# One encoder kernel: the front of each layer issued by a list scheduler in the builder, and group A's rope and softmax scaling moved to DVE

## The chip, the core and the metric

The kernel runs on one core of one Trainium2 chip. A core has five engines with queues of their own, each of which takes its instructions strictly in the order in which the built program puts them: PE (matrix multiplies, with the weight loads shown as PEld), DVE (element-wise work and reductions), ACT (activations and copies), POOL (element-wise work on SBUF alone) and SP (here the queue that issues the DMAs). Matrix products land in PSUM, which has eight banks of 128 x 512 f32; everything else lives in SBUF. The metric is the device time of one launch in microseconds (us); the time given for a kernel is the median of its runs.

## What is computed

Two layers of an encoder over 512 positions of width 1024, in f32. Each layer is a front (norm, projections, two kinds of attention, output projection) and a mixer (gated MLP with a short convolution):

```python
for l in range(DEPTH):                                   # 2 layers
    h = rmsnorm(x, g_attn[l])
    qa, ka, va, qb, kb, vb = split(h @ w_in[l])          # 1024 -> 2304 columns
    qa, ka, qb, kb = (rope(rmsnorm_per_head(t)) for t in (qa, ka, qb, kb))
    ya = windowed_gqa_sink(qa, ka, va, sink[l])          # group A: 8 q heads, 2 kv heads, +/-128 keys
    yb = diff_attention(qb, kb, vb, lam)                 # group B: 4 heads, two softmaxes each, all keys
    yb = rmsnorm(yb, subln[l]) * (1.0 - lambda_init)
    x = x + concat(ya, yb) @ w_out[l]
    h = rmsnorm(x, g_ffn[l])
    gate, val = split(h @ w_up[l])
    x = x + (silu(conv3(gate)) * val) @ w_down[l]
```

## The kernel before

**Products in three parts.** Every operand of a large product is held as a rounded high part and a low remainder, and `mm3` (L200) issues three matmuls for one product: high by high, high by low, low by high. A high part is made by a copy on ACT, the low part by a subtraction on DVE or POOL (`split`, L189; `split_out` for results that come from PSUM). Weights arrive as units of up to 512 KB: one DMA, one copy on ACT, one subtraction; units of the later projections and of the output projection have the subtraction on POOL, the first four projection chunks and the mixer on DVE. Up to three units are prepared ahead of their use.

**The front.** The input projection has nine chunks of 256 columns (`CHUNKS`): `akv`, `aq0`, `aq1` for group A, then `bq`, `bk`, `bv` for each half of group B. In `project` a chunk runs as two token pairs `tp` of 48 matmuls each (`pj_aq`, `pj_bq` ... in the profile). A finished q or k chunk goes through `qk_out`: ACT copies and squares (`raw`, `sq`), DVE reduces the squares (L354), POOL takes the reciprocal root (L245), the rotated half is multiplied (L366, on DVE for A and on POOL for B), POOL multiplies by the cosine table (L371) and adds (L372), DVE scales a k chunk (L374), and PE transposes into the one `tq` bank (`tr_ka`, `tr_qa`, `tr_bq`, `tr_bk`), from which high and low parts are made.

**Group A** has eight blocks (head pair `ip`, query block `qb`). `a_scores` makes two sets of scores (`sc_a`, PE), masks them and takes maxima on DVE (L451), then the exponentials (L469) and the scaling by the reciprocal sum (L476), both on ACT, into four `so_a` tiles of the eight `tmp` buffers. `a_values` transposes the probabilities (`pt_a`), splits them and multiplies by the values (`pv_a`).

**Group B** has 16 blocks (half, `qb`, head `j`). `b_scores` makes two sets of scores into the single two-bank buffer `sc` (`sc_b`), DVE takes the maxima (L539), ACT the two exponentials (L543), and DVE combines both maps into one (L547 to L551). `b_weights` transposes (`wt_b`) and splits (`wh_b`, `wl_b`), `b_values` multiplies by the values into the one `acc` bank (`yb`), and `b_norm` does the per-head norm of a pair of heads: a sum of squares on PE (`ss_yb`), a reciprocal root on POOL (`rr_yb`), a broadcast on PE (`rt_yb`), a multiplication on DVE (L603) and a split.

**The output projection** runs in passes as its inputs become ready: `out_pass(0)` over group A's rows (`wo`, 96 matmuls of 512 columns), `out_pass(1)` over the first half of B (48), and `out_last` over the second half of B in two token halves (`wo`, 48 matmuls of 256 columns each); the last of them, `out_last(1)`, cannot begin before the last `b_norm`.

**What sets the order.** `akv`, `aq0` and `aq1` run one after another. Then `weave` takes steps from two tracks, the attention (`attend`) and the rest (`proj_b(0)`, `proj_b(1)`, the output passes), so that both advance in proportion to two fixed totals, `ATT` = 92.0 and 98.6. Within `attend` the values of a block follow the scores of the next (group A) or next but one (`LAG` = 2, group B). The tile framework then sorts all instructions by priority against a modelled timeline of its own and writes each engine's queue; where the builder asks for it, `high_priority` moves group A's scores ahead.

## Time and profile before

| | us |
|---|---|
| median of 3 runs | 1272.37 (1271.11 to 1274.77) |
| the profiled execution | 1273.49 |
| its span in the trace | 1271.7 |
| PE, DVE, ACT, POOL busy in that span | 1228.0, 722.4, 573.5, 348.6 |

"Busy" counts a matmul from its start until its modelled end, and matmuls overlap, so that PE shows as busy while a short wait or a slower clock passes; the clock that PE was granted stands apart, as PEclk. A front begins in layer 0 at 19.2 us of the span, where the first `pj_aq` follows the chunk `akv` that was computed while `x` was loaded, and ends at 276.5 us, where the first `up` matmul starts. In layer 1 it goes from 640.4 us, the first `pj_akv`, to 904.6 us, the last `wo`.

### The profile page before, as it was taken

What the parts mean: (1) busy time and instruction counts of PE and PEld (TensorE: products, weight loads), DVE (VectorE), ACT (ScalarE), POOL (GpSimd) and SP (SyncE); (2) the same over time, 40 slices, a digit from 0 to 9 for tenths busy, and PEclk for the clock granted to TensorE, in tenths of its full rate; (3) what the DMA queues carried; (4) which work ended last, traced back from release to release, by engine and by line L of the source; (5) the groups of instructions that cost most, each with busy time, mean ns of one, the idle gap of its engine ahead of it and who ended that gap; (6) DMA issues with size and microseconds to landing.
All of it is one profiled execution on the core that took longest, in us unless ns stands there. A gap on an engine that the chain in (4) does not pass through costs nothing. (4 is left out here: it accounts for less than half of the span.)

```text
span 1271.7 us, 17055 instructions
## 1 busy us (share of the span) xinstructions
PE 1228.0 (97%) x6644; PEld 1035.9 (81%) x6644; DVE 722.4 (57%) x1186; ACT 573.5 (45%) x1011; POOL 348.6 (27%) x348
## 2 busy tenths in 40 slices
PE   9989997899999999999999899988999999999998
PEld 8879975688888888888898889867888888888887
DVE  6665677776655335554456667766865543355532
ACT  5487754444433223333444787554444332233321
POOL 1894641133111000112157647412321100011100
PEclk9999997999999999999999899979999999999999
DMA  6211220113332333322332212101133323333232
GB/s 210 68 51 51 59 67 17 34 51 100 106 95 82 100 107 106 91 89 84 106 89 62 66 35 67 51 17 50 50 116 99 100 75 99 108 99 100 81 110 91
DMA packets 33616, 102.92 MB, mean 81 GB/s; under 512 B 3968, under 2 KB 5248, under 8 KB 33536
## 3 DMA queue, kind: packets, MB, share of 16 engines
q1 hardware_dynamic: 33536, 101.84, 26.4%
q8 instruction: 52, 0.85, 0.3%
q14 instruction: 28, 0.23, 0.1%
HBM read 99.73 MB, written 2.10 MB: 80 GB/s over the span
## 5 line engine op out<-in xcount | busy, mean ns | idle before, releaser
L190 ACT CAST wh<-wr 128x1024 fp32r<-128x1024 f32 (+2 forms) x202 | 195.0, 967 | 401.6 <-PE up L202 171.4
L202 PE MATMUL up<-nf_l,wh 128*128 128x512 f32 x704 | 274.6, 390 | 0.6 <-DVE nf_l L220 0.5
L203 PE MATMUL up<-nf_h,wl 128*128 128x512 f32 x704 | 274.1, 390 | 0.4
L201 PE MATMUL up<-nf_h,wh 128*128 128x512 f32 x704 | 273.5, 390 | 0.0
L191 DVE TENSOR_TENSOR wl<-wr,wh 128x1024 fp32r<-128x1024 f32 (+2 forms) x166 | 185.5, 1118 | 105.9 <-ACT wh L190 105.6
L741 POOL TENSOR_TENSOR cv<-cv,rb 128x512 f32<-128x512 f32 x44 | 59.1, 1345 | 516.3 <-ACT cv L740 516.3
L202 PEld LDWEIGHTS up<-nf_l,wh 128*128 128x128 f32 x704 | 132.2, 188 | 30.0 <-DVE nf_l L220 2.8
L203 PEld LDWEIGHTS up<-nf_h,wl 128*128 128x128 f32 x704 | 132.2, 188 | 28.7 <-DVE wl L191 1.5
L201 PEld LDWEIGHTS up<-nf_h,wh 128*128 128x128 f32 x704 | 132.2, 188 | 27.3 <-ACT nf_h L219 0.2
L201 PE MATMUL dn<-act,wh 128*128 128x512 f32 x352 | 138.4, 394 | 0.0
L203 PE MATMUL dn<-act,wl 128*128 128x512 f32 x352 | 137.7, 392 | 0.0
L202 PE MATMUL dn<-act,wh 128*128 128x512 f32 x352 | 136.3, 388 | 0.0
L191 POOL TENSOR_TENSOR wl<-wr,wh 128x1024 fp32r<-128x1024 f32 x36 | 86.6, 2411 | 98.6 <-ACT wh L190 79.5
L734 DVE TENSOR_TENSOR gp<-up,rb 128x512 f32<-128x512 f32 x44 | 30.3, 692 | 104.1 <-PE up L203 98.8
L203 PEld LDWEIGHTS dn<-act,wl 128*128 128x128 f32 x352 | 66.1, 188 | 15.5
L202 PEld LDWEIGHTS dn<-act,wh 128*128 128x128 f32 x352 | 66.1, 188 | 14.8
L201 PEld LDWEIGHTS dn<-act,wh 128*128 128x128 f32 x352 | 66.2, 188 | 13.2
L742 DVE TENSOR_TENSOR cv<-cv,up 128x512 f32<-128x512 f32 x44 | 30.2, 686 | 81.1 <-POOL cv L741 71.8
L543 ACT ACTIVATE e_b<-sc_b,mx_b,rqb 128x512 f32<-128x512 f32 x64 | 49.3, 776 | 41.0 <-DVE mx_b L540 36.0
L755 DVE TENSOR_TENSOR x<-x,dn 128x512 f32<-128x512 f32 x32 | 22.1, 689 | 76.4 <-PE dn L203 76.4
L740 ACT ACTIVATE cv<-cv 128x512 f32<-128x512 f32 x44 | 27.7, 632 | 71.6 <-DVE cv L739 71.6
L539 DVE TENSOR_REDUCE mx_b<-sc_b 128x2 f32<-128x1024 f32 x32 | 39.0, 1220 | 10.0 <-PE sc_b L537 9.8
(224 smaller groups left out, 2545.3 us busy)
## 6 DMA issues: line engine op xcount, KB each, us to landing
wr<-w_up SPq DMA_DIRECT2D x88, 512.0 KB, 3.6
wr<-w_in SPq DMA_DIRECT2D x34, 512.0 KB, 3.7
wr<-w_down SPq DMA_DIRECT2D x32, 384.0 KB, 3.0
wr<-w_down SPq DMA_DIRECT2D x32, 320.0 KB, 2.9
wr<-w_out SPq DMA_DIRECT2D x16, 512.0 KB, 3.7
x<-xT SPq DMA_DIRECT2D x8, 256.0 KB, 4.4
outT<-x SPq DMA_DIRECT2D x8, 256.0 KB, 2.0
prob_f<-w_in SPq DMA_DIRECT2D x8, 128.0 KB, 4.3
```

The source lines that it names most:

```text
L190: nc.scalar.copy(hi, raw)
L191: eng.tensor_tensor(out=lo, in0=raw, in1=hi, op=ALU.subtract)
L201: nc.tensor.matmul(acc, lhsT=a[0], rhs=b[0], start=start, stop=False)
L202: nc.tensor.matmul(acc, lhsT=a[0], rhs=b[1], start=False, stop=False)
L203: nc.tensor.matmul(acc, lhsT=a[1], rhs=b[0], start=False, stop=stop)
L539: nc.vector.tensor_reduce(out=mx, in_=scp, axis=AX, op=ALU.max)
L543: nc.scalar.activation(e[c], sc[c], AF.Exp, bias=mx[:, c:c + 1], scale=rq[:, c:c + 1], accum_out=lsum[:, c:c + 1])
L734: nc.vector.tensor_tensor(out=g[:, 1:S + 1], in0=acc[0], in1=rb, op=ALU.mult)
L740: nc.scalar.activation(cv, cv, AF.Silu)
L741: nc.gpsimd.tensor_tensor(out=cv, in0=cv, in1=rb, op=ALU.mult)
L742: nc.vector.tensor_tensor(out=cv, in0=cv, in1=acc[1], op=ALU.mult)
L755: nc.vector.tensor_tensor(out=x_sb[d], in0=x_sb[d], in1=acc, op=ALU.add)
```

## The change

The front of each layer is put out by a list scheduler in the builder. A clock `clk` advances by an estimated time for each piece of PE work that a track yields; `pause` lets a track wait for an estimated time, `when` for names that `mark` has put a time to. Buffers of one kind are such names too: the score buffer (`sc`), the two transpose banks (`at0`, `at1`), `acc` and `tq`. `pump` always takes the ready track of the lowest rank. Chains behind a finished bank (`qk_out`, `a_soft`, `b_soft`, `copy_out`, `b_norm`, `add_x`) are spawned as tracks of rank 0, the values of all blocks are one track of rank 1, the scores of all blocks one of rank 2, and a track of rank 3, `filler`, holds all projections and output passes. So filler is issued only where nothing else is ready by the estimate. `proj_b(1)` starts once all of group A's scores are out.

Three things change beside the order. In `qk_out` group A's cosine product and addition go from POOL to DVE. In the softmax of A the four scalings go from ACT's `activation` to DVE's `tensor_scalar`. `wt_b` always uses the `at` banks, and the first projection pairs of a layer use the `mm` banks alone. The framework's own sorting stays on; the `high_priority` block is gone.

```diff
-    def weave(*tracks):
...
+    def when(*names):
+        return lambda: max(due.get(n, never) for n in names)
+
+    def mark(name, dt=0.0):
+        due[name] = clk["now"] + dt
+
+    def spawn(rank, gen):
+        tracks.append([rank, gen, lambda: 0.0])
+
+    def pump():
+        while tracks:
+            ready = [v for v in tracks if v[2]() <= clk["now"]]
+            if not ready:
+                clk["now"] = min(v[2]() for v in tracks)
+                assert clk["now"] < never
+                continue
+            tr = min(ready, key=lambda v: v[0])
+            step = next(tr[1], None)
+            if step is None:
+                tracks.remove(tr)
+            elif callable(step):
+                tr[2] = step
+            else:
+                clk["now"] += step
+                tr[2] = lambda: 0.0
...
-            rsqrt(rs, sv)
+            cv = tab[:, 0, t2].unsqueeze(2).broadcast_to([P, 2, nh, HD])
             tb = sq
+            eng = nc.vector if on_dve else nc.gpsimd
             for i in range(2):
...
-            cv = tab[:, 0, t2].unsqueeze(2).broadcast_to([P, 2, nh, HD])
-            nc.gpsimd.tensor_tensor(out=heads(raw), in0=heads(raw), in1=cv, op=ALU.mult)
-            nc.gpsimd.tensor_tensor(out=raw, in0=raw, in1=tb, op=ALU.add)
+            eng.tensor_tensor(out=heads(raw), in0=heads(raw), in1=cv, op=ALU.mult)
+            eng.tensor_tensor(out=raw, in0=raw, in1=tb, op=ALU.add)
+            rsqrt(rs, sv)
+            if on_dve:
+                yield pause(0.6 + 2.8 * n / CW)
+            else:
+                due["POOL"] = max(clk["now"] + 1.0, due["POOL"]) + 1.6 + 2.6 * n / CW
+                t = due["POOL"] + 0.2
+                yield lambda: t
...
             for i in range(4):
-                nc.scalar.activation(so[i][:, :n], so[i][:, :n], AF.Copy, scale=rl[:, i:i + 1])
+                nc.vector.tensor_scalar(out=so[i][:, :n], in0=so[i][:, :n], scalar1=rl[:, i:i + 1], scalar2=None,
+                                        op0=ALU.mult)
             a_so[ip, qb] = so
+            mark(f"so{ip}{qb}", 4 * (0.15 + 0.5 * n / S))
...
-        def attend():
...
+        def all_scores():
+            for ip, qb in a_seq:
+                yield from a_scores(ip, qb)
+            mark("a_scored")
+            for half, qb, j in b_seq:
+                yield from b_scores(half, qb, j)
...
         def proj_b(half):
+            if half:
+                yield when("a_scored")
...
+        def filler():
+            yield from first_part()
+            yield from proj_b(0)
+            yield from proj_b(1)
+            yield from out_pass(0, mm)
+            yield from out_pass(1, mm)
+            yield when("yb10")
             w_last.extend([next_unit(), next_unit()])
             yield from out_last(0, w_last, mm)
 
-        weave((attend(), ATT),
-              (chain(proj_b(0), proj_b(1), out_pass(0, mm), out_pass(1, mm), out_tail()), 98.6))
+        spawn(2, all_scores())
+        spawn(1, all_values())
+        spawn(3, filler())
+        pump()
         run(out_last(1, w_last, wide))
```

**PE, layer 0, group B's second half.** `sc_b_2_0` are the scores of head 2, query block 0; `wt_b_2_0` the transposes of its combined map. Before, the queue held at this place:

```order
L563 MATMUL wt_b_2_0_2568<-ident,e_b_2_0_0_2432 128x128 x4
L537 MATMUL sc_b_3_0_2528<-bkh_1_1607,bqh_1_1605 128x512 x2
L537 MATMUL sc_b_3_0_2528<-bkl_1_1608,bqh_1_1605 128x512 x2
L537 MATMUL sc_b_3_0_2528<-bkh_1_1607,bql_1_1606 128x512 x2
L593 MATMUL ss_yb_0_1_2575<-unit,sq_yb_0_1_2523 128x1 x4
L563 MATMUL wt_b_2_1_2624<-ident,e_b_2_1_0_2479 128x128 x4
L537 MATMUL sc_b_3_1_2600<-bkh_1_1607,bqh_1_1605 128x512 x2
L537 MATMUL sc_b_3_1_2600<-bkl_1_1608,bqh_1_1605 128x512 x2
L537 MATMUL sc_b_3_1_2600<-bkh_1_1607,bql_1_1606 128x512 x2
```

Now, around the first scores of that half (`wo_0_3` and `wo_0_4` are outputs 3 and 4 of `out_pass(0)`, 12 matmuls each):

```order
L224 MATMUL wo_0_3_2555<-yh_1_321,wl_2196 128x512
L628 MATMUL sc_b_2_0_2450<-bkh_1_1702,bqh_1_1700 128x512 x2
L628 MATMUL sc_b_2_0_2450<-bkl_1_1703,bqh_1_1700 128x512 x2
L628 MATMUL sc_b_2_0_2450<-bkh_1_1702,bql_1_1701 128x512 x2
L222 MATMUL wo_0_4_2600<-yh_0_319,wh_2201 128x512
L223 MATMUL wo_0_4_2600<-yl_0_320,wh_2201 128x512
L224 MATMUL wo_0_4_2600<-yh_0_319,wl_2202 128x512
```

Before, outputs 0 to 4 of `out_pass(0)` stood ahead of this place, none between the five score sets `sc_b_1_3`, `sc_b_2_0`, `sc_b_2_1`, `sc_b_3_0` and `sc_b_3_1`, and outputs 5 to 7 behind it; now outputs 2 to 7 stand between those sets.

**POOL, layer 0, the rope of group A.** `rs_ka` and `rqa` are reciprocal roots, `raw_kv` and `raw_qa` the rope's products and sums, `tab_3` a table for group B. Before:

```order
L245 TENSOR_TENSOR rs_ka_0_370<-sv_ka_0_368,unit 128x4
L371 TENSOR_TENSOR raw_kv_0_359<-raw_kv_0_359,tab_1_293 128x2x128
L245 TENSOR_TENSOR rs_ka_1_405<-sv_ka_1_403,unit 128x4
L372 TENSOR_TENSOR raw_kv_0_359<-raw_kv_0_359,sq_ka_0_364 128x2x128
L371 TENSOR_TENSOR raw_kv_1_394<-raw_kv_1_394,tab_1_293 128x2x128
L372 TENSOR_TENSOR raw_kv_1_394<-raw_kv_1_394,sq_ka_1_399 128x2x128
```

Now:

```order
L266 TENSOR_TENSOR rs_ka_0_399<-sv_ka_0_397,unit 128x4
L266 TENSOR_TENSOR rs_ka_1_429<-sv_ka_1_427,unit 128x4
L313 TENSOR_TENSOR tab_3_721<-rope_sb,rows_291 128x256
L317 TENSOR_TENSOR tab_3_721<-rope_sb,rows_291 128x4x32 x2
L266 TENSOR_TENSOR rqa_313<-sv_qa_0_488,unit 128x2x4
L266 TENSOR_TENSOR rqa_313<-sv_qa_1_558,unit 128x2x4
```

The products and sums of `raw_kv` and `raw_qa` have left POOL's queue and stand in DVE's.

**PE, layer 0, the end of the front.** `ss_yb_1_1` and `rt_yb_1_1` belong to the last norm. Before, two outputs of `out_pass(1)` stood between them (`wo_1_6` and `wo_1_7`, six rows each, of which the first three are shown; `rt_yb_1_1` follows):

```order
L203 MATMUL wo_1_5_2973<-yh_b_2337,wl_2641 128x512
L593 MATMUL ss_yb_1_1_2956<-unit,sq_yb_1_1_2952 128x1 x4
L201 MATMUL wo_1_6_2981<-yh_b_2337,wh_2640 128x512
L202 MATMUL wo_1_6_2981<-yl_b_2338,wh_2640 128x512
L203 MATMUL wo_1_6_2981<-yh_b_2337,wl_2641 128x512
```

Now (`wo_2_1_0` is the first output of `out_last(1)`):

```order
L224 MATMUL yb_1_1_2913<-wh_b_3_2_2927,vb_1_1_2420 128x256
L711 MATMUL ss_yb_1_1_3057<-unit,sq_yb_1_1_3051 128x1 x4
L725 MATMUL rt_yb_1_1_3065<-ident,rr_yb_1_1_3062 128x128 x4
L807 MATMUL wo_2_1_0_3073<-yh_b_2877,wh_2680 128x256 x2
L807 MATMUL wo_2_1_0_3073<-yh_b_2877,wl_2681 128x256 x2
```

The last norm's three steps on PE now follow each other with no other PE work between them, and `out_last(0)` stands ahead of the last values instead of behind the norm.

More of the change, by code (lines that the diff above doesn't have):

```diff
@@ L123, in chain, with pause @@
             yield from g
-    def weave(*tracks):
-        live = [[g, total, 0.0, None] for g, total in tracks]
-        while live:
-            free = [v for v in live if v[3] is None or v[3]()]
-            tr = min(free, key=lambda v: v[2] / v[1])
-            try:
-                step = next(tr[0])
-                tr[3] = step if callable(step) else None
-                if tr[3] is None:
-                    tr[2] += step
-            except StopIteration:
-                live.remove(tr)
+    never = 1e9
+    clk = {"now": 0.0}
+    due = {}
+    tracks = []
+    def pause(dt):
+        t = clk["now"] + dt
+        return lambda: t
+    def when(*names):
[20 more added lines that the diff above has]
+                tr[2] = lambda: 0.0
     x_sb = [const.tile([P, S], F32, name=f"x{k}") for k in range(NK)]
@@ L316 @@
                                 op0=ALU.subtract, op1=ALU.subtract)
-        if l:
-            r_tok = norm.rms()
+        due.clear()
+        used = {"tmp": 0, "chain": 0}
+        for n in ("sc", "at0", "at1", "acc", "tq", "POOL"):
+            mark(n)
         h_in = norm
+        rt_box = [None]
         def project(name, done, alloc):
@@ L455, in a_scores @@
-            yield 2.0
+            for i in range(2):
+                yield when("sc")
+                due["sc"] = never
+                scp = sc2(f"sc_{nm}_{i}")
+                sc = (scp[:, 0], scp[:, 1])
+                for j, (u, v) in enumerate(((0, 0), (0, 1), (1, 0))):
+                    for g in range(2):
+                        rs = slice(g * HD, (g + 1) * HD)
+                        nc.tensor.matmul(sc[g][:, :n], lhsT=q[u][rs, i, qb * P:(qb + 1) * P],
+                                         rhs=k[v][rs, kb0 * P:kb1 * P], start=j == 0, stop=j == 2)
+                for g in range(2):
+                    s = tmp(f"so_{nm}_{i}_{g}")
+                    nc.vector.tensor_tensor_reduce(out=s[:, :n], in0=sc[g][:, :n], in1=mask_sb[:, m0:m0 + n],
+                                                   op0=ALU.add, op1=ALU.max, scale=1.0, scalar=-3.0e38,
+                                                   accum_out=mx[:, 2 * i + g:2 * i + g + 1])
+                    so.append(s)
+                yield 0.9 * n / S + 0.1
+                mark("sc", 3.0 * n / S)
@@ L576, in b_values @@
                 if b % 2:
-                    yield 0.7
+                    yield 0.73
         def b_norm(half, qp):
@@ L597, in b_norm @@
             rsqrt(rr, rr)
-            yield 0.5
+            mark("tq", 0.4)
+            yield pause(1.7)
+            yield when("tq")
+            due["tq"] = never
             rt = tq(f"rt_{nm}")
@@ new lines, in b_norm @@
+            yield from copy_out(yh, yl, y.rearrange("p (j q) -> p j q", j=2), f"yb{half}{qp}")
+        a_seq = [(ip, qb) for ip in range(2) for qb in range(NT)]
+        b_seq = [(half, 2 * qp + i, j) for half in range(2) for qp in range(2) for j in range(2) for i in range(2)]
+        def all_scores():
[4 more added lines that the diff above has]
+                yield from b_scores(half, qb, j)
@@ L629, in values, with all_values @@
+        def all_values():
+            for ip, qb in a_seq:
+                yield from a_values(ip, qb)
+            for half, qb, j in b_seq:
+                yield from b_weights(half, qb, j)
                 if qb % 2:
-                    yield lambda: ("values", kind) in qk
-                    yield from b_values(kind, qb // 2, j)
+                    yield from b_values(half, qb // 2, j)
                     if j:
-                        g = b_norm(kind, qb // 2)
-                        yield next(g)
-                        norms.append(g)
@@ L660, in proj_b, with add_x @@
+                f"bq{half}{tp}")), mm)
+            yield from project(f"bk{half}", lambda bank, tp: spawn(0, qk_out(
+                scaled(f"raw_bk{half}{l}_{tp}", bank, tp), tp, tabs[3], qk[half][1], f"bk{half}", None,
+                f"bk{half}{tp}")), mm)
             yield from project(f"bv{half}", lambda bank, tp: bv_done(half, bank, tp), mm)
-            qk["values", half] = True
+            mark(f"vb{half}", 2.0)
         norm = Norm(l, c0, f"nf{l}")
+        def add_x(d, acc, o):
+            yield pause(0.3)
+            nc.vector.tensor_tensor(out=x_sb[d][:, o], in0=x_sb[d][:, o], in1=acc, op=ALU.add)
```

265 lines of the change are left out of this document (153 added, 112 removed).

## The prediction

> **What bounds the kernel now.** I read the page first: its busy times, then PE's slices and the granted clock below them.
>
> ```profile
> PE 1228.0 (97%) x6644; PEld 1035.9 (81%) x6644; DVE 722.4 (57%) x1186; ACT 573.5 (45%) x1011; POOL 348.6 (27%) x348
> ...
> PE   9989997899999999999999899988999999999998
> ...
> PEclk9999997999999999999999899979999999999999
> ```
>
> PE is the bound, and looks almost full. But the two digits below 8 in PEclk fall into slices 7 and 27, the attention of both layers: there PE waits so often that its clock drops. The mixers show nothing but nines. So I took both fronts by themselves (columns: stretch, length, busy time and count of PE, PEld, DVE, ACT, POOL, then PEclk, DMA share, GB/s):
>
> ```profile
> 19.20:276.50 257.30, 236.08 (x1627) 206.47 (x1625) 173.47 (x374) 152.40 (x334) 123.97 (x93) 0.95 0.17 53
> 640.40:904.60 264.20, 248.04 (x1724) 217.77 (x1722) 177.07 (x368) 153.13 (x331) 123.38 (x88) 0.95 0.18 53
> ```
>
> How long would PE need if it never waited? Each kind of matmul has a place where it runs back to back at clock 1.00. Single-tile windows show (stretch, length, PE busy and count), in this order, 256-column projections, 512-column products, a set of B scores, four transposes, A scores of 256 and of 384 keys, and a norm's broadcast:
>
> ```profile
> 19.20:30.40 11.20, 11.20 (x94) 1.00 0.36 100
> ...
> 1218.00:1266.00 48.00, 48.00 (x211) 1.00 0.37 114
> ...
> 228.53:229.43 0.90, 0.90 (x6) 1.00 0.00 0
> ...
> 103.91:104.26 0.35, 0.35 (x4) 1.00 0.00 0
> ...
> 92.96:93.51 0.55, 0.55 (x6) 1.00 0.22 37
> 128.80:129.53 0.73, 0.73 (x6) 1.00 0.00 0
> ...
> 263.78:264.60 0.82, 0.82 (x8) 1.00 0.00 0
> ```
>
> So 0.119 us per 256-column matmul and 0.2275 per 512-column one. Layer 0's front has 960 of the first (768 projection, 96 `yb`, 96 `out_last`), 204 of the second (144 `wo`, 60 `pv_a`), 16 B score sets, 8 + 8 A sets, 196 transposes and nine small norm steps: 114.2 + 46.4 + 14.4 + 10.2 + 17.2 + 7.4 = 209.8. It takes 257.3, so 47 are lost; layer 1, with 96 more projections, needs 221.2 of 264.2 and loses 43. About 90 us is all that any order of the front can win.
>
> Where is it lost?
>
> ```profile
> 37.40:97.00 59.60, 52.49 (x391) 48.09 (x389) 40.03 (x97) 37.94 (x86) 52.12 (x41) 0.94 0.16 49
> 97.00:168.60 71.60, 71.60 (x548) 64.75 (x548) 46.30 (x120) 55.33 (x134) 42.64 (x31) 1.00 0.18 55
> 168.60:225.60 57.00, 47.38 (x249) 36.54 (x247) 39.61 (x72) 27.95 (x59) 11.54 (x6) 0.82 0.12 38
> 225.60:276.50 50.90, 46.41 (x296) 38.90 (x293) 34.57 (x66) 20.01 (x37) 9.71 (x5) 1.00 0.14 42
> ...
> 670.40:736.00 65.60, 60.88 (x454) 55.16 (x453) 43.39 (x100) 43.03 (x98) 44.18 (x33) 0.95 0.17 53
> 736.00:803.80 67.80, 66.64 (x507) 59.79 (x506) 49.36 (x110) 51.33 (x122) 39.86 (x28) 1.00 0.16 47
> ...
> 829.00:856.30 27.30, 21.43 (x103) 15.81 (x102) 18.25 (x36) 13.89 (x29) 1.98 (x2) 0.69 0.01 5
> 856.30:904.60 48.30, 44.24 (x273) 37.73 (x273) 31.42 (x61) 17.57 (x33) 8.19 (x5) 0.96 0.14 44
> ```
>
> Counting each stretch's matmuls at the prices above gives the lost time. **Projections with group A** (first two rows of each layer): 14 + 4 in layer 0, 12 + 6 in layer 1, in all 36. **Group B after the projections** (168.6 to 225.6; 803.8 to 856.3, of which the row from 829 holds 14 of 16): 21 + 16 = 37. **The last blocks and the end**: 7 + 8 = 15.
>
> **The change, part by part: group B.** What releases PE there, in the timeline of the bare stretch:
>
> ```profile
> 214.74 0.80 PE L537 MATMUL sc_b<-bkh,bqh 64*128 64x512 f32 x2 [2.59 <-ACT e_b L543]
> ...
> 216.43 1.23 DVE L539 TENSOR_REDUCE mx_b<-sc_b 128x2 f32<-128x1024 f32 x1 [0.45 <-PE sc_b L537]
> ...
> 217.97 0.78 ACT L543 ACTIVATE e_b<-sc_b,mx_b,rqb 128x512 f32<-128x512 f32 x1 [2.22 <-DVE mx_b L540]
> ...
> 218.74 0.77 ACT L543 ACTIVATE e_b<-sc_b,mx_b,rqb 128x512 f32<-128x512 f32 x1
> ...
> 219.65 0.79 PE L537 MATMUL sc_b<-bkh,bqh 64*128 64x512 f32 x2 [0.51 <-ACT e_b L543]
> ...
> 220.71 0.74 DVE L551 SCALAR_TENSOR_TENSOR e_b<-e_b,al_b,e_b 128x512 f32<-128x512 f32 x1
> 221.37 1.22 DVE L539 TENSOR_REDUCE mx_b<-sc_b 128x2 f32<-128x1024 f32 x1
> ```
>
> There is one score buffer, so a set waits for the maxima and both exponentials of the set before: 219.65 - 214.74 = 4.9 us from set to set, about 4.2 if the scores run at full clock. The combined map ends at 221.45, some 5 us after its scores (which end at about 216.3). A block therefore costs no PE time only if other PE work of about 3.3 us lies between one set's end and the next, and 5 us between a set and its transposes. Before, five sets stood almost bare. In the new order I counted the work between the starts of successive sets in layer 0, from the eleventh back to the fifth: 9.0, 6.8, 6.8, 7.8, 8.3, 8.3 us; in layer 1 none of the same gaps is under 4.8. So the single buffer no longer binds until the last four or five sets. What remains is what woven stretches lose even so: 4 of 71.6 and 6 of 67.8 above, so 3.5 per layer. Gain 37 - 7 = **30**, between 20 (if DVE and ACT answer half as promptly as the rows) and 33.
>
> **Group A's start.** Prices and waits (first the rows of the moved operations: count, shortest/median/longest ns; then PE's waits from 36 to 97 us):
>
> ```profile
> L371 POOL TENSOR_TENSOR raw_qa<-raw_qa,tab x8: 1272/1289/1942, 45.7 to 686.5; 128x512 f32<-128x512 f32 x8
> L374 DVE TENSOR_TENSOR raw_bk<-raw_bk,rs_bk x8: 679/686/2872, 95.6 to 799.6; 128x512 f32<-128x512 f32 x8
> L366 DVE TENSOR_TENSOR sq_qa<-raw_qa,tab x16: 410/419/2593, 43.8 to 684.9; 128x256 f32<-128x256 f32 x16
> L476 ACT ACTIVATE so_a<-so_a,rl_a x64: 492/566/618, 67.3 to 775.5; 128x256 f32<-128x256 f32 x32, 128x384 f32<-128x384 f32 x32
> ...
> PE pj_bk L201 <- ACT raw_bq L342: 3.2, 1, 3.2
> PE sc_a L447 <- DVE mx_a L451: 1.5, 1, 1.5
> ```
>
> A q pair's product and sum cost 2 x 1.29 on POOL and 2 x 0.69 on DVE: each of the four chains per layer is 1.2 us shorter, and POOL, 52.1 of 59.6 us busy there, loses some 13 us per layer (4 x 2.58, and 2 x 1.3 for the k chains of half the width). DVE gains 4 x 1.38 + 2 x 0.7 = 7. The 32 scalings per layer take 18 us off ACT (32 x 0.566). On DVE no row shows them: with one f32 input they lie between nothing and the two-input row of 0.42 for 256 columns, about 0.55 for 384. I take that row: at most 16 us per layer.
>
> [...]
>
> DVE's load in layer 0's stage from 37.4 to 168.6 becomes 40.0 + 46.3 + 7 + 16 = 109 us, against PE work of 113 (131.2 less the 18 lost). A queue that is 97% full cannot answer everywhere in time. I put the loss halfway between what woven work shows (4 of 67 us, so 7 of 113) and the present 18: 12.5 per layer. There is also a stretch without filler: between `bv` of the first half and `bq` of the second, layer 0's PE now has 7 us of bare A blocks. Gain 36 - 25 = **11**, from -10 (below) to 29 (woven throughout).
>
> **The end.** Before, `out_pass(1)` covered the last norm; now most filler is spent by then. Durations of the norm's steps:
>
> ```profile
> L245 POOL TENSOR_TENSOR rr_yb<-rr_yb,unit x8: 1006/1009/1503, 197.5 to 888.9; 128x4 f32<-128x4 f32 x8
> ...
> L603 DVE TENSOR_TENSOR y_yb<-y_yb,rt_yb x8: 676/680/689, 200.4 to 892.5; 128x512 f32<-128x512 f32 x8
> ...
> L190 ACT CAST yh_b<-y_yb x8: 612/621/625, 201.2 to 893.2; 128x512 fp32r<-128x512 f32 x8
> ...
> PE yb L201 <- ACT wh_b L190: 1.4, 2, 0.7
> ...
> PE yb L202 <- DVE wl_b L191: 0.3, 1, 0.3
> ```
>
> From one engine to the next some 0.15 us pass (exponential to 219.51, scores from 219.65 above). Behind the last `yb`, PE waits for a square on ACT (0.62 like the copy, + 0.15), between `ss_yb` and `rt_yb` for a small DVE step and POOL (1.0, and about 0.6 with the hand-overs), then for the multiplication and the copy (0.68 + 0.62 + 0.3): 4.0. Three `yb` blocks follow their transposes at once; two waited 1.7 in all from 168.6 to 276.5 us (last two rows), so 0.85 each: 2.6. Two sets closer than 3.3 us, and the transposes behind them, 1.6; an earlier norm 0.8. That is 9.0; the waits lie so close that I add 3 for a slower clock (0.69 in the bare stretch above): 12 per layer, 24 against 15. Change **-9**, from -16 to -2. The mixers are untouched.
>
> Sum: 30 + 11 - 9 = 32 us. The profiled execution took 1273.5 (span 1271.7 and 1.8 around it), the median is 1.1 less: 1272.4 - 32 = **1240**.
>
> **Rivals.** *DVE becomes the bound of group A's stage.* For it, two rows (first DVE's, then POOL's):
>
> ```profile
> 51.62 2.93 DVE L366 TENSOR_TENSOR sq_qa<-raw_qa,tab 128x256 f32<-128x256 f32 x2
> ...
> 51.64 2.63 POOL L191 TENSOR_TENSOR wl<-wr,wh 128x1024 fp32r<-128x1024 f32 x1
> ```
>
> Two products of 0.42 took 2.93 while POOL ran one subtraction of 2.63, and the second went on only as POOL ended. The change puts 12 more two-input operations and eight groups of four scalings per layer on DVE. If each of these 20 places waits half of a POOL subtraction, 72% of the time (POOL's 95 of 131 us, less 13, over 113), that is 20 x 0.9 = 17 us more: 126 on DVE against 113 on PE, a loss of 13 and the 5 or so that woven work has anyway, 18 per layer as now. Then 30 + 0 - 9 = 21, so **1251**.
>
> [...]
>
> *Slower.* The same place at full price: if each of the 20 waits the 2.2 us that the row shows (2.59 - 0.42), DVE carries 109 + 43 = 152 us, the stage loses 39 instead of 18 per layer, and 30 - 42 - 9 = -21: **1293**. It decides from about 1.6 us per place. Against it: POOL's own load falls by 13 us, and most rows of L366 stand at the median of 0.42.
>
> *Fully woven:* A's stage loses 7 and B's 2 per layer, the end 9: 36 - 14 + 37 - 4 + 15 - 18 = 52, so **1220**.
>
> *The order does not hold:* the estimates in the builder are off and the waits only move elsewhere, a sum near nothing: **1272**. The queues show the filler spread, which speaks against it.
>
> **How the numbers follow.** Forecast 0.55 (its own range 1230 to 1248), DVE-bound 0.20, fully woven 0.12, order not holding 0.05, slower 0.08. The range takes in 1220 and 1251 with the bounds of A's and B's terms: 1217 to 1262. A change of less than 0.3% (3.8 us) could not be told from none. Faster 0.87, same 0.05, slower 0.08.
>
> **What would show it.** In the new trace: `sc_b` sets at least 5 us apart without PE waiting for `e_b` until the last four, PEclk 1.00 through group B and dropping only at the end, where `rt_yb` and `wo` wait about 4 us; POOL near 110 us per front, DVE 188 to 196; layer fronts of about 239 and 250 us. Wrong would be: PE waiting for `so_a`, `raw_qa` or `mx_a` for more than 12 us per layer, or many scalings and rope products of over 1 us.

## The result and the profile after

The changed kernel takes **1281.6 us** (median of 4 runs, 1280.9 to 1282.5), the kernel before 1273.6 beside it: a ratio of **1.0066, 95% interval 1.0049 to 1.0083**. It is slower by 8 us, where 1240 us, 32 less than before, were forecast. The profiled execution took 1282.45.

The page of the changed kernel, the lines that answer those shown of before:

```profile
span 1280.6 us, 17036 instructions
...
PE 1232.3 (96%) x6644; PEld 1037.4 (81%) x6644; DVE 757.1 (59%) x1274; ACT 546.2 (43%) x947; POOL 322.5 (25%) x324
...
PE   9897999889999999999999999998899999999998
...
PEclk9898999979999999999999999999899999999999
```

The engines' loads moved as the change says: DVE up by 35 us, POOL down by 26, ACT by 27. But PEclk has not become a row of nines. The two dips of before, slices 7 and 27, are gone; new ones stand in slices 2, 4, 9 and 29. The stretches of both fronts, cut at the first score set of group A, the first of B and B's eleventh (stretch, length, busy time of PE, PEld, DVE, ACT, POOL, then PEclk, DMA share, GB/s):

```profile
19.90:52.60 32.70, 29.34 (x225) 29.00 (x223) 24.66 (x50) 18.60 (x35) 16.05 (x18) 0.90 0.27 81
52.60:144.20 91.60, 80.07 (x576) 69.57 (x575) 76.31 (x193) 52.05 (x130) 42.16 (x29) 0.94 0.16 47
144.20:224.30 80.10, 79.68 (x533) 68.20 (x532) 57.75 (x101) 46.76 (x96) 46.52 (x30) 1.00 0.20 63
224.30:287.35 63.05, 51.92 (x298) 44.06 (x298) 38.74 (x77) 22.26 (x46) 8.19 (x5) 0.84 0.08 26
652.50:684.50 32.00, 32.00 (x269) 31.87 (x267) 21.14 (x42) 16.02 (x29) 11.24 (x12) 1.00 0.33 98
684.50:773.30 88.80, 85.96 (x634) 75.80 (x633) 71.87 (x195) 55.18 (x133) 44.32 (x32) 0.98 0.16 48
773.30:855.00 81.70, 79.76 (x525) 66.93 (x523) 57.80 (x98) 45.49 (x95) 45.62 (x28) 1.00 0.20 59
855.00:911.70 56.70, 48.41 (x298) 40.35 (x298) 37.38 (x76) 22.95 (x46) 8.19 (x6) 0.91 0.09 29
```

The kernel before, by the same cuts:

```profile
19.20:54.55 35.35, 32.94 (x260) 32.16 (x258) 26.35 (x45) 18.41 (x34) 24.29 (x26) 0.95 0.30 90
54.55:144.03 89.48, 84.78 (x645) 76.62 (x645) 55.29 (x159) 68.34 (x164) 61.29 (x45) 0.98 0.18 56
144.03:214.74 70.71, 61.60 (x385) 50.34 (x384) 51.26 (x92) 40.90 (x90) 27.67 (x18) 0.93 0.15 47
214.74:276.50 61.76, 56.76 (x341) 47.35 (x341) 40.57 (x80) 24.75 (x48) 10.71 (x6) 0.92 0.12 34
640.40:674.00 33.60, 33.60 (x282) 33.47 (x280) 17.94 (x34) 16.12 (x29) 21.52 (x20) 1.00 0.32 94
674.00:770.74 96.74, 90.86 (x676) 81.42 (x675) 65.91 (x161) 70.20 (x165) 58.52 (x40) 0.96 0.17 50
770.74:841.02 70.28, 65.22 (x425) 54.38 (x424) 51.73 (x94) 41.68 (x92) 33.18 (x22) 0.94 0.18 53
841.02:904.60 63.58, 58.36 (x343) 48.50 (x343) 41.49 (x81) 25.13 (x48) 10.17 (x6) 0.91 0.11 34
```

In the changed kernel B's first ten sets (third and seventh rows) run at clock 1.00 with PE nearly full, as forecast. What lies in front of them in layer 0, and behind them in both layers, does not. Layer 0's front became 10 us longer (267.4 instead of 257.3), layer 1's 5 us shorter (259.2 instead of 264.2). The other 4 us are a later first `pj_aq` (0.7) and waits at the start of the two mixers (1.2 and 1.8).

Counting matmuls at the prediction's prices in each stretch gives the lost time, here for both layers together, with the same cuts in both kernels:

| lost, us | projections and A | B's first ten sets | the rest of the front | sum |
|---|---|---|---|---|
| before | 33.7 | 29.3 | 26.5 | 89.5 |
| after | 42.6 | 13.1 | 39.7 | 95.4 |

So B's middle lost 16 less than before, and A and the end lost 9 and 13 more. PE's longest waits in layer 0's front (waiting operation and its releaser: us in total, times, longest):

```profile
PE pt_a L568 <- DVE so_a L538: 4.6, 5, 1.5
PE pv_a L223 <- DVE p_a L546: 4.4, 1, 4.4
PE pj_aq L222 <- ACT raw_kv L366: 3.4, 1, 3.4
PE wt_b L672 <- DVE e_b L653: 3.3, 3, 2.3
```

**The 4.4 us.** First DVE around it, then POOL, then PE, in time (start, duration):

```profile
112.57 5.35 DVE L538 TENSOR_SCALAR so_a<-so_a,rl_a 128x256 f32<-128x256 f32 x4
117.84 1.28 DVE L546 TENSOR_TENSOR p_a<-pt_a,p_a 128x512 fp32r<-128x512 f32 x2
```

```profile
113.07 4.70 POOL L212 TENSOR_TENSOR wl<-wr,wh 128x1024 fp32r<-128x1024 f32 x2 [8.23 <-ACT wh L211]
```

```profile
113.66 0.50 PE L222 MATMUL pv_a<-p_a,va 128*128 128x512 f32 x1 [0.39 <-ACT p_a L544]
118.57 0.79 PE L223 MATMUL pv_a<-p_a,va 128*128 128x512 f32 x1 [4.42 <-DVE p_a L546]
```

Four scalings took 5.35 us instead of 1.4: the first two 0.35 each, the other two 2.47 and 2.42 while POOL subtracted two weights beside them, in 4.70. The low part `p_a` was queued behind on DVE, and PE waited for it. All 64 scalings (columns after the count: busy us, mean ns, idle before them):

```profile
L538 DVE TENSOR_SCALAR so_a<-so_a,rl_a 128x256 f32<-128x256 f32 (+1 forms) x64 | 39.1, 672 | 0.2
```

and by duration (ns: shortest, median, longest; first and last start):

```profile
L538 DVE TENSOR_SCALAR so_a<-so_a,rl_a x64: 337/410/2555, 69.5 to 778.6; 128x256 f32<-128x256 f32 x32, 128x384 f32<-128x384 f32 x32
```

The median is 0.41 us, the mean 0.67: twelve of the 64 took over 1 us.

**The stretch without filler.** From 112.5 to 131.1 us layer 0's PE has A's blocks alone, about 7 us of work in 18.6. The next filler, `bq` of B's second half, cannot start sooner, because its bank still holds `bv`, whose matmuls ended at 112.5 but whose reading stands in the queues of ACT and DVE behind A's exponentials:

```profile
126.98 0.84 ACT L430 ACTIVATE vb<-pj_bv,na_r 128x256 fp32r<-128x256 f32 x2
```

```profile
130.13 0.48 DVE L431 SCALAR_TENSOR_TENSOR vb<-pj_bv,na_r,vb 128x256 fp32r<-128x256 f32 x1
```

In PE's own queue `bq` also stands behind A's transposes, which end at 130.9 us, so it could not start sooner unless both came sooner.

**The end.** Windows of 4 us over layer 0's last norm (columns as above):

```profile
262.00:266.00 4.00, 3.64 (x31) 3.43 (x29) 3.05 (x7) 2.22 (x5) 0.00 (x0) 1.00 0.00 0
266.00:270.00 4.00, 2.40 (x17) 1.79 (x16) 2.64 (x8) 0.59 (x1) 0.00 (x0) 1.00 0.00 0
270.00:274.00 4.00, 3.25 (x17) 2.96 (x18) 0.00 (x0) 1.18 (x2) 0.00 (x0) 0.57 0.00 0
274.00:278.00 4.00, 2.64 (x11) 2.26 (x11) 0.16 (x1) 0.00 (x0) 1.01 (x1) 0.50 0.00 0
278.00:282.00 4.00, 2.52 (x12) 2.52 (x12) 1.38 (x2) 0.62 (x1) 0.00 (x0) 0.50 0.00 0
282.00:286.00 4.00, 4.00 (x27) 4.00 (x27) 1.51 (x5) 1.06 (x2) 0.00 (x0) 0.73 0.00 0
```

After three waits of 0.3 to 0.7 us (the second row) the clock falls to one half, in the middle of `yb` at 270.5 us, and stays there for 13.7 us, the last 4.7 of them without a wait. `out_last(1)`, 48 matmuls that take 5.7 us at full clock, takes 7.9. In the last stretch of both fronts together PE's waits add up to 19.4 us of the 39.7 lost. PE was busy there for 25.6 us at half clock (16.9 and 8.7); matmuls of 256 columns start 0.21 us apart at that clock and 0.12 at full clock, so by estimate the slow clock cost some 11 us. The other 9 are in neither. Part of them may be waiting too, since a wait counts only from the modelled end of the matmul before it, 0.28 us after its start at full clock.

When did the clock fall? In the 4 us from 266 to 270 (the second row), the last whole row at clock 1.00, PE was busy for 2.40; the clock came back at 284.2 us, within a row in which PE was busy throughout (the last). Whether the length of the waits or the share of the time that PE was busy decided it, no run separates.

### The profile page after: what moved, and what is told of

It is laid out like the page before. It is cut to its first block, busy times and chain, and to the rows that moved or that the text cites. A ratio compares the mean times of both kernels' runs of the same rounds, so it can differ in the third digit from the quotient of the medians.

```text
span 1280.6 us, 17036 instructions
## 1 busy us (share of the span) xinstructions
PE 1232.3 (96%) x6644; PEld 1037.4 (81%) x6644; DVE 757.1 (59%) x1274; ACT 546.2 (43%) x947; POOL 322.5 (25%) x324
```

## The experiments

All runs stand beside runs of the kernel before on the same chip, whose medians were 1272.5 to 1273.7 us. One thing has to be known to read them. The framework sorts each engine's queue anew for every version, so an edit of one engine moves PE's queue too. PE's matmuls agree with the changed kernel's up to the 241st in the run with another bank, the 470th with the scalings on ACT, the 340th with the weights on DVE, of 6554. None of these is the same order with one price changed.

| version | median us | ratio to before, 95% | A | B's first ten | rest | lost in all |
|---|---|---|---|---|---|---|
| before | 1273 | | 33.7 | 29.3 | 26.5 | 89.5 |
| after | 1281.6 | 1.0066 (1.0049 to 1.0083) | 42.6 | 13.1 | 39.7 | 95.4 |
| scale_act | 1274.8 | 1.0013 (1.0003 to 1.0023) | 44.5 | 9.8 | 33.2 | 87.5 |
| order_alone | 1283.0 | 1.0069 (1.0056 to 1.0082) | 46.7 | 9.2 | 41.6 | 97.5 |
| est_14 | 1282.0 | 1.0063 (1.0045 to 1.0080) | 42.3 | 14.5 | 38.8 | 95.6 |
| bank_sc | 1273.9 | 1.0003 (0.9992 to 1.0015) | 41.4 | 12.9 | 32.7 | 87.0 |
| act_bank | 1277.8 | 1.0042 (1.0023 to 1.0061) | 44.4 | 9.4 | 39.9 | 93.7 |
| low_dve | 1273.7 | 1.0013 (0.9999 to 1.0026) | 35.6 | 11.2 | 40.0 | 86.8 |
| pace | 1308.2 | 1.0291 (1.0267 to 1.0314) | 43.0 | 38.5 | 41.2 | 122.7 |
| before_dve | 1277.9 | 1.0052 (1.0032 to 1.0073) | 34.9 | 30.1 | 28.1 | 93.1 |
| lean_out | 1269.4 | 0.9977 (0.9964 to 0.9989) | 41.6 | 21.1 | 34.9 | 97.6 |
| low_bank | 1270.6 | 0.9977 (0.9965 to 0.9988) | 32.5 | 13.0 | 36.6 | 82.1 |
| gate_low_bank | 1277.3 | 1.0037 (1.0023 to 1.0050) | 17.4 | 35.4 | 38.7 | 91.5 |
| low_act | 1284.4 | 1.0088 (1.0072 to 1.0104) | 44.1 | 16.2 | 37.8 | 98.1 |
| warm_end | 1277.6 | 1.0042 (1.0024 to 1.0061) | 42.1 | 12.6 | 37.3 | 92.0 |
| low_bank_warm | 1260.8 | 0.9917 (0.9897 to 0.9937) | 31.7 | 10.2 | 34.1 | 76.0 |
| low_before | 1265.4 | 0.9950 (0.9933 to 0.9968) | 21.8 | 35.2 | 26.2 | 83.2 |
| low_before_dve | 1282.3 | 1.0075 (1.0056 to 1.0095) | 18.5 | 46.7 | 28.2 | 93.4 |
| low_bank_warm2 | **1259.2** | **0.9895 (0.9876 to 0.9914)** | 32.5 | 10.1 | 30.7 | 73.3 |

Each version is explained below, under its label. The last four columns are us of the profiled execution, both layers, counted as above; the extra matmuls of the three "warm" versions count as lost.

### The scalings on ACT; the order alone

```diff
-                nc.vector.tensor_scalar(out=so[i][:, :n], in0=so[i][:, :n], scalar1=rl[:, i:i + 1], scalar2=None,
-                                        op0=ALU.mult)
+                nc.scalar.activation(so[i][:, :n], so[i][:, :n], AF.Copy, scale=rl[:, i:i + 1])
```

> The changed kernel with A's 64 scalings back on ACT as before; rope stays on DVE and the builder's estimates stay as they are. Theory D (the scalings on DVE, blocked while POOL subtracts weights, are what A's stage of layer 0 lost): the waits for so_a and the 4.4 us wait for p_a at 114 us go, with the cold clock behind them, 1270 to 1276 us. Theory S (the builder's times for A are too short, so the filler runs out before A does, and the engine of the scalings hardly matters): within 3 us of the changed kernel's 1281.6, and the stretch of A without filler at 112 to 131 us stays.

`scale_act`: 1274.8 us, as theory D expected in size. But A's stage lost no less (44.5 against 42.6). The stretch without filler stayed, with other waits in it, and the 8 us less stand in B and behind it. So the size supports D, and the place does not.

Besides this edit, the second version has the rope on POOL again:

```diff
-            eng = nc.vector if on_dve else nc.gpsimd
+            eng = nc.gpsimd
```

> The changed kernel with both A's scalings on ACT and A's rope on POOL, as before: the new order alone. Theory D: POOL and ACT carry again what they did, DVE is free; the order is worth what I forecast for group B, 1255 to 1270 us. Theory S: the order itself is what loses, 1281 to 1290 us, since each of A's q chains is also 1.2 us longer.

`order_alone`: 1283.0 us, S's figure. **The new order by itself, its choice of banks included, makes the kernel 9 us slower on the old engines.** Between this run and the one above lies the rope alone: 8 us better on DVE. One wait fits that: in `order_alone` PE waits 2.2 us for `raw_qa` from POOL at 61 us, the longest of the start but one. That it explains the whole is not shown, since PE's queues in the two differ from the 241st matmul on.

### Longer times for A in the builder

```diff
-        t = clk["now"] + dt
+        t = clk["now"] + dt * stretch["f"]
...
-        due[name] = clk["now"] + dt
+        due[name] = clk["now"] + dt * stretch["f"]
...
+        stretch["f"] = 1.4
```

The factor goes back to 1.0 where A's last scores are put out.

> The changed kernel with every wait time that the builder assumes in A's stage multiplied by 1.4, until A's last scores are put out; B's times and all engines unchanged. Theory S: filler stands beside all of A's sets, the 12 us lost at 112 to 131 us in layer 0 and some of the 8 us lost at 736 to 773 us in layer 1 go, 1265 to 1273 us. Theory D: the scalings go on blocking, the place of the wait only moves, 1279 to 1285 us.

`est_14`: 1282.0 us, no change. Filler does stand beside the last A sets now (`bq` from 113 us on), but the loss in A is the same, and DVE's scalings are blocked elsewhere: PE waits 3.7 us for `p_a` at 115.5 us. So S's mechanism, estimates that are too short, does not explain by itself what A's stage loses.

### The banks at the start of layer 0

```diff
-            yield from proj_a(1, mm)
+            yield from proj_a(1, mm if l else lambda nm: (lambda n: sc2(n)[:, 0], mm)[int(nm[-1])](nm))
```

> The changed kernel with aq1's first pair of layer 0 in the banks of the scores, as before, and not in an mm bank. Theory E (the 3.4 us wait for raw_kv at 32 us and the cold clock behind it, 6.5 us, lie on the path): 1274 to 1277 us. Rival (A's own chain sets when B starts, so an earlier start of the projections is waited out later): 1280 us or more.

`bank_sc`: 1273.9 us, theory E. The wait of 3.4 us for `raw_kv` is gone, and the stretch before A's first scores loses 1.8 instead of 6.7 us. That is 5 of the 8 us. The rest lies in another listing of what follows: A's sets in layer 0 lost 3.6 more, the end of layer 0 10.6 less, the end of layer 1 3.6 more.

> The changed kernel with A's scalings on ACT and with aq1's first pair of layer 0 in the banks of the scores: the two edits that gave 7 and 8 us one by one, together. If each removes a loss of its own: 1265 to 1269 us. If both only shorten the same stretch of A in layer 0 (its stage is then set by what is left): 1272 to 1276 us.

`act_bank`: 1277.8 us, neither. **The two edits, worth 7 and 8 us alone, give 4 together.** The gain at the start is there (1.8 us lost), and the end gives back what each had won there (39.9 against 33.2 and 32.7).

### B's sets closer together

```diff
-            yield pause(1.6)
+            yield pause(1.0)
             e = []
...
-            mark("sc", 2.1)
+            mark("sc", 1.2)
```

> The changed kernel with the builder's two waiting times between B's score sets shortened (1.6 to 1.0 and 2.1 to 1.2 us), so that it puts out sets about 4 to 6 us apart instead of 7 to 8; nothing else. Theory P (B's sets are put out too far apart, so the filler is spent before B's last sets, and those stand bare): the loss after B's tenth set, 23.0 and 16.7 us in the two layers, falls to about 12 each, 1265 to 1270 us. Rival (the chip's own chain of a set, scores to scores, needs the 7 to 8 us, or the second half of B waits for its projections anyway): 1278 to 1285 us, with PE waiting between the sets instead of behind them.

`pace`: 1308.2 us, 27 worse than the changed kernel, and far beyond the rival. The sets of the second half cannot start before `bk` of that half has gone through its chain. With B's first half out sooner, most of the output pass was spent as filler in front of that point: 30 us lie between the last set of the first half (194.8 us) and the first of the second (224.8), where the changed kernel has 7, and 30 `wo` matmuls in a row follow before the next set. That the sets stand too far apart is not refuted by this; only that shorter times in the builder bring them nearer.

### The weights' subtraction off POOL

```diff
-        eng = nc.gpsimd if kind in ("inb", "out") else nc.vector
+        eng = nc.vector
```

> The changed kernel with the subtraction of every front weight on DVE (about 1.23 us each there) and no longer on POOL (2.4 us each); scalings and rope of A stay on DVE. Theory L (what hurts is DVE standing still while POOL subtracts: 14 of 64 scalings took 1.3 to 2.6 us, 18.7 us in all): the long scalings vanish, and in spite of some 42 us more work on DVE per layer the time is 1270 to 1279 us. Rival (DVE is simply full): the scalings get short, but PE waits more for DVE in A's stage, 1285 to 1305 us.

`low_dve`: 1273.7 us, theory L. The scalings of this version:

```profile
L538 DVE TENSOR_SCALAR so_a<-so_a,rl_a 128x256 f32<-128x256 f32 (+1 forms) x64 | 24.8, 449 | 0.2
```

39.1 us fell to 24.8, and three of 64 are over 1 us instead of twelve (the expectation's 14 was a miscount). A's stage lost 35.6 instead of 42.6. DVE is not too full for 1.23 us per weight. That DVE stands still while POOL subtracts, as it did for 2.47 and 2.42 us at 113 us beside subtractions of 4.70 in all, is the "lock" of the expectations that follow.

> The changed kernel with the weights' subtraction on DVE and A's scalings on ACT. Theory L (both edits remove the same thing, scalings that stand still while POOL subtracts): no more than either alone, 1272 to 1277 us. Rival (each removes load of its own): 1265 to 1269 us.

`low_act`: 1284.4 us, far off both. With the weights off POOL, the scalings are better on DVE, by 11 us; with the weights on POOL they are better on ACT, by 7. Most of the 11 stand in A (44.1 against 35.6), where PE waits on ACT again (3.8 us for `p_a` at 125 us). Which part is ACT's load and which the new listing was not separated.

> The changed kernel with the weights' subtraction on DVE and with aq1's first pair of layer 0 in the scores' banks: two edits worth 8 us each one by one. If the lock between DVE and POOL and the bank each cost a time of their own: 1264 to 1268 us. If the sum is lost again, as it was with the scalings on ACT (1277.8 where 1267 was expected): 1272 to 1280 us, and PE's loss only moves behind A's stage.

`low_bank`: 1270.6 us, between the two; the second edit is worth 3 here. This version is **faster than before by 0.2%** (0.12 to 0.35%).

### More filler beside A

To `low_bank`'s edits this adds the stretched times and an earlier start of the second half's `bq`:

```diff
             if half:
-                yield when("a_scored")
+                yield when("a_half")
...
                 yield from a_scores(ip, qb)
+                if (ip, qb) == (0, NT - 1):
+                    mark("a_half")
```

`bk` of the second half still waits for all of A's scores.

> As the run with both the weights' subtraction on DVE and the scores' banks, and besides with A's assumed times stretched by 1.4 and the q projection of B's second half let in after A's first half instead of after all of A's scores. More filler then stands beside A and less beside B. Theory C (B's chain and A's chain set the length, filler moved from one to the other is worth nothing beyond the places left bare): A's stage loses 10 us less, B's second half 10 more, 1268 to 1280 us. Rival (bare stretches in A were the main loss): 1255 to 1262 us.

`gate_low_bank`: 1277.3 us, theory C. A's stage lost 17.4 us instead of 32.5, as little as I had hoped for, and B's first ten sets 35.4 instead of 13.0. **Filler moved ahead uncovers what it covered before.**

### Less work on PE

```diff
-                    mm3(acc, (w[0][:, kk, :], w[1][:, kk, :]), (y_hi[k0 + k], y_lo[k0 + k]), k == 0, k == nk - 1)
+                    if p == 0:
+                        nc.tensor.matmul(acc, lhsT=w[0][:, kk, :], rhs=y_hi[k], start=k == 0, stop=False)
+                        nc.tensor.matmul(acc, lhsT=w[0][:, kk, :], rhs=y_lo[k], start=False, stop=k == nk - 1)
...
```

> The changed kernel without the third product (low weights by high values) of the first out pass, 32 matmuls of 512 columns less per layer, 7.3 us of PE work each, 14.6 in all; the output lacks that term. Theory C (from group B's second half on the front is as long as B's own chain of sets and the last norm, and filler only fills it): the time falls by less than 5 us, 1277 to 1281, and PE waits more behind it. Rival (PE's work sets the front's length): 1266 to 1269 us.

`lean_out`: 1269.4 us, 12.2 less for 14.6 us of work. Theory C is wrong in this form. B's chain does not set the length: where filler is taken away, the sets behind it come sooner, and the loss stays nearly what it was (97.6 against 95.4).

### Matmuls that keep the clock

```diff
+            if (half, qp) == (1, 1):
+                spare = sc2(f"spare{l}")
+                for i in range(6):
+                    nc.tensor.matmul(spare[:, 0, i % 4 * P:i % 4 * P + P], lhsT=sq[:, i % 4 * P:i % 4 * P + P], rhs=ident,
+                                     start=True, stop=True)
...
+            if (half, qp) == (1, 1):
+                for i in range(6):
+                    nc.tensor.matmul(spare[:, 1, i % 4 * P:i % 4 * P + P], lhsT=rr[:, i % 4:i % 4 + 1].broadcast_to([P, P]),
+                                     rhs=ident, start=True, stop=True)
```

> The changed kernel with twelve matmuls of 128 columns more per layer, whose results nobody reads, six behind the last norm's sums and six behind its transposed factors; they fill PE's two waits there (1.34 and 1.50 us; six take 1.28 even at half clock). Theory K (half of what the end loses is the half clock that follows waits, matmuls of 256 columns 0.21 us apart where they were 0.12 from 270.6 to 284 us): out_last(1) runs at full clock, 2 to 4 us less per layer, 1273 to 1278 us. Rival (the clock does not answer to so little work, or only the waits count): 1280 to 1284 us.

`warm_end`: 1277.6 us, 4 less and inside K's range. The profile shows that I had priced it wrongly. The same place in layer 0, in time (start, duration, count):

```profile
271.97 1.86 PE L711 MATMUL ss_yb<-unit,sq_yb 128*128 128x1 f32 x8 [0.75 <-ACT sq_yb L698]
273.70 2.91 PE L715 MATMUL spare<-ident,sq_yb 128*128 128x128 f32 x12
276.40 1.92 PE L730 MATMUL rt_yb<-ident,rr_yb 128*128 128x128 f32 x8
278.11 2.04 PE L734 MATMUL spare<-ident,rr_yb 128*128 128x128 f32 x12
279.90 0.48 PE L816 MATMUL wo<-yh_b,wh 128*128 128x256 f32 x2
```

Six such f32 matmuls are twelve records of 0.22 us at half clock, 2.7 us and not 1.28 (the 1.28 was my estimate, six at some 0.21), and overrun the wait by 1.3. The clock comes back before `wo` (0.72 from 277 to 281 us, then 1.00; 5.7 us for the 48, instead of 7.9), but layer 0, whose PE queue is otherwise the same, gains nothing in all (63.1 against 63.0). The gain is layer 1's, where the end took 54.3 instead of 56.7 where the queue differs from the first `up` blocks of layer 0 on.

> The run with the weights' subtraction on DVE and the scores' banks (1270.6), with the same twelve matmuls. Theory K: 1263 to 1267 us. Rival: 1269 to 1273 us.

`low_bank_warm`: 1260.8 us, 10 below `low_bank`, more than K expected. Again layer 0, in the same queue, has none of it (its last stretch 58.2 instead of 57.1); layer 1 got better in all stretches, by 2.2, 1.6 and 3.6 us, in a queue that differs from the first `up` blocks of layer 0 on. So only a part of it can be put down to the clock.

The last version puts eight more ahead, where PE waited behind the last transposes and inside the last values:

```diff
+                for b in range(NT):
+                    nc.tensor.transpose(spare[:, 0, b * P:(b + 1) * P], w[:, b * P:(b + 1) * P], ident)
...
+                for b in range(4):
+                    nc.tensor.matmul(b_st["spare"][:, 1, :CW], lhsT=vh, rhs=wt[0][:, 3], start=True, stop=True)
```

> As the run at 1260.8 us, with eight more such matmuls per layer, in the two waits behind the last set's transposes and the last values. Theory K: the half clock at the end goes altogether, 1 to 2 us less per layer, 1257 to 1259 us. Rival (they stand in the way of the values by as much): 1260 to 1263 us.

`low_bank_warm2`: **1259.2 us, 1.05% faster than before** (0.86 to 1.24%), K's range. This is the clean comparison: layer 0's queue on PE is that of `low_bank` and `low_bank_warm` but for these matmuls, and layer 1's is that of `low_bank_warm`. Layer 0's end:

```profile
257.85 0.28 PE L224 MATMUL yb<-wh_b,vb 128*128 128x256 f32 x1
258.87 1.05 PE L718 MATMUL ss_yb<-unit,sq_yb 128*128 128x1 f32 x8 [0.75 <-ACT sq_yb L705]
259.79 1.58 PE L722 MATMUL spare<-ident,sq_yb 128*128 128x128 f32 x12
261.26 1.16 PE L737 MATMUL rt_yb<-ident,rr_yb 128*128 128x128 f32 x8
262.26 1.50 PE L741 MATMUL spare<-ident,rr_yb 128*128 128x128 f32 x12
263.92 0.50 PE L823 MATMUL wo<-yh_b,wh 128*128 128x256 f32 x2 [0.16 <-ACT yh_b L544]
```

The norm's sums (four f32 matmuls, eight records) begin within 1 us of the last `yb` and take 1.05 us, where the changed kernel needs 1.86 at clock 0.50; `rt_yb` takes 1.16 instead of 2.07. No row here has the times of the half clock. The page of `low_bank_warm` gives the clock in the slice around this place, 252 to 284 us, as 8 tenths; the mean clock of the whole execution is 0.989 there, 0.992 here and 0.979 in the changed kernel. The stretch took 54.8 us; it was 58.2 with twelve extra matmuls and 57.1 with none. So keeping the clock is worth 2.3 us there, although the stretch holds twenty matmuls more. Most of the rest of the gain over `low_bank` stands in layer 1, whose queue is another, and is not shown to be the clock's. Layer 1, where the first twelve had kept the clock already (9 tenths or more in every slice from 284 us on, on the page of `low_bank_warm`), gained nothing further (55.9 after 56.0).

### The engines in the old order

> The kernel before, in its old weave, with A's scalings and A's rope product and sum on DVE: the second half of the change alone. Theory D (blocked scalings cost, rope gains): the two nearly cancel, 1271 to 1277 us. Theory F (my forecast: shorter chains and a free ACT are worth something by themselves): 1262 to 1268 us.

`before_dve` (both moves made in the kernel before: scalings and rope on DVE): 1277.9 us, just above D's range and far from F's. By themselves the moves make the kernel 5 us worse. The scalings took up to 2.6 us on DVE, and PE waited for them (`so_a`) 5.2 us in layer 0.

> The kernel before with nothing changed but the subtraction of the front's weights, on DVE instead of POOL. If the lock between the two engines cost there as much as in the changed kernel: 1262 to 1267 us. If it costs only where A's scalings stand on DVE: 1271 us or more, since DVE gets some 42 us more work per layer.

`low_before` (one line, as in `low_dve`): 1265.4 us, **0.5% faster than before** (0.32 to 0.67%). It is also 5 us faster than `low_bank`, the new order's best version with neither extra nor missing matmuls. DVE's operations had been held up in the kernel before already; the product behind B's maxima, first before, then in this version (busy us, mean ns, idle before them):

```profile
L540 DVE SCALAR_TENSOR_TENSOR mx_b<-mx_b,rqb 128x2 f32<-128x2 f32 x32 | 15.2, 474 | 0.7
...
L540 DVE SCALAR_TENSOR_TENSOR mx_b<-mx_b,rqb 128x2 f32<-128x2 f32 x32 | 6.1, 191 | 0.5
```

POOL has 36 subtractions of 2.4 us less to do as well, so its own chains are a rival cause that was not separated.

> The kernel before in its old weave, with A's scalings and rope on DVE as in the change, and the weights' subtraction on DVE too: the same engines as the run at 1273.7 us, in the old order. Theory O (the new order gains nothing by itself, the engines were the useful half once the lock is gone): 1258 to 1265 us, so the old order is 9 us or more better. Rival (the new order gains what group B shows in the middle): 1274 us or more.

`low_before_dve`: 1282.3 us, as the rival had it. On the same engines, with the weights on DVE, the old order is 9 us worse than the new; with scalings on ACT, rope and weights on POOL it is 9 us better. **What an order is worth depends on the engines it was made for.** Here, too, the loss was moved: A's stage lost 18.5 instead of 34.9, B's first ten sets 46.7 instead of 30.1.

## Why the prediction was wrong

The prediction left 25 us of loss to A, 7 to B's middle and 24 to the end, 56 in all. The changed kernel lost 42.6, 13.1 and 39.7, 95.4 in all. (The cuts lie a little otherwise: before, the loss is 89.5 us by these and 88 by the prediction's.) Two steps failed most, the loss of A's stage by 18 us and that of the end by 16. Point by point:

**Group B, +30: mechanism right, size wrong.** As forecast, the first ten sets stand 7 to 9 us apart (once 11.5, in layer 1), PE waits there for `e_b` no longer than 0.4 us in either layer, and the clock is 1.00. The loss in them fell from 29.3 to 13.1 us, 16 in place of what I had counted as most of 30. Woven work lost 5.2 and 7.9 per layer, not 3.5.

**The end, -9: the loss was 40, not 24.** By the same cuts it lost 13 more than before. I had named the waits well: the last norm's three are 0.75, 1.34 and 1.5, where I had 4.0 for them, and all waits of the stretch are 11.1 and 8.3 us in the two layers, where I had 9.0. Then I added "3 for a slower clock" per layer, and the half clock cost by estimate some 7.5 in layer 0 and 4 in layer 1; some 9 us more were in no term of mine, and their cause stays open. B and the end together gave 3 us; 21 were forecast. The filler that filled B's middle was missing behind it, which the step "most filler is spent by then" saw and priced too low.

**Group A's start, +11: the sign was wrong, and this is the largest miss.** It was -9, some 20 us off the forecast. The step reads: "I put the loss halfway between what woven work shows (4 of 67 us, so 7 of 113) and the present 18: 12.5 per layer". Layer 1 lost 13.3, close to that. Layer 0 lost 29.3, and three things show in its trace. The first pair of `aq1` got an `mm` bank that still held `akv` (3.4 us of waiting, 5 with the clock; `bank_sc` removed it); I had read that the early pairs use the `mm` banks alone, and had not asked when those come free. Scalings stood still while POOL subtracted weights (`low_dve` got 7 us back in this stage). And the stretch without filler, which I noted as "7 us of bare A blocks" and gave no price, took 18.6 us. The wait of 4.4 us behind blocked scalings falls into that stretch, so the three overlap.

**What the forecast left out:** 3.7 us of a later start and of waits at the start of the mixers.

**The load terms held.** DVE was busy for 197 and 188 us per front (188 to 196 forecast), POOL for 113 and 109 (110). The loads did not decide anything.

**The rivals.** *DVE as A's bound* had the right mechanism and the wrong measure. I counted 17 us per layer of blocked time; the 64 scalings took 14 us longer in both layers together than in `low_dve`. Its largest single wait came by place, one block of four in front of a `p_a` that PE needed. *The order does not hold* came nearest in time (1272), and its phrase "the waits only move elsewhere" is what the runs show; it had 0.05. The slower rival's price, 2.2 us at each of 20 places, was paid at few. So the side was forecast wrongly with a weight of 0.08, because each rival was one mechanism and the result is three small ones.

*What a scaling costs.* The two that stood still at 113 us took 2.47 and 2.42 us, as long as the subtractions beside them (4.70 for two). Unblocked medians are 0.348 us for 256 columns and 0.414 for 384, so 0.52 ns per further column; the two-source product and sum took 0.419 for 256 and 0.69 for 512, 1.06 ns. The whole operation is only a sixth shorter for 256 columns, since by estimate from the two widths some 0.2 us of it do not grow with the columns; my 16 us per layer were 12 where nothing blocked.

**What stays open.** The edits do not add up: scalings on ACT gain 7 with the weights on POOL and lose 11 with them on DVE; the bank is worth 8 alone and 3 on top of `low_dve`. Each edit also had PE's queue listed anew, and no run held that queue fixed while one engine's price changed. How much of any single difference of up to 10 us is the edit and how much the new listing is not settled.

## What to carry to other kernels

When a reordering fills the bare places of one stage, count what the filler covered before: over 14 of the 17 other versions the loss in the fronts stayed between 82 and 98 us while it moved from stage to stage by up to 20, and the two below that are those from which three causes together were removed (DVE standing still beside POOL, a bank held too long, a clock that falls). Where several waits on PE lie within a few microseconds, price the slower clock beside them: at the end of these fronts it came to some 11 us beside 19.4 us of waits. A cheap operation on a free engine is dear if it stands still beside another engine's work in front of something that the busiest engine waits for (here four scalings took 5.35 us instead of 1.4, and PE waited 4.4); so ask of each move which instruction is queued behind it, not how full the engine is.

## What the runs showed that was not expected

- The clock fell to one half, at 270.5 us, although none of PE's waits in the 10 us before was longer than 0.7 us. From 266 to 270 us PE was busy for 2.40 of 4; the clock came back at 284.2 us, 4.7 us after the work was continuous again.
- Extra matmuls whose results nobody reads paid for themselves where the half clock stayed away (`low_bank_warm2`, 54.8 against 57.1 us of a stretch), and did not where they came after it had fallen (`warm_end`, 63.1 against 63.0).
- The norm's f32 matmuls of 128 columns stand in the traces as two records each: at clock 1.00 the four `rt_yb` are eight records in 0.82 us (before), and at 0.50 the six extra ones are twelve in 2.7 us (`warm_end`).
- Not only large operations stand still beside POOL's subtractions. The 128x2 product behind B's maxima has a median of 0.15 us, and in the changed kernel took 2.43 at 156.1 us, beside a subtraction of 2.40.
